# Storing part of one chunk through a second DMA queue, in a fused LoRA linear layer on one core

## The chip, the core and the metric

The kernel runs on one core of one Trainium2 chip. The metric is the device time of one execution in microseconds; the time before is the median of three runs.

## The reference

The inputs are `x` (16 x 2048 x 256, float32), a weight `W` (256 x 256), a low-rank pair `lora_A` (256 x 16) and `lora_B` (16 x 256), a vector `lora_E` of 16 and a scalar `scale`, which is 1.0.

```python
x_flat = x.reshape(-1, in_dim)              # 32768 x 256
y = x_flat @ W
lora_out = x_flat @ lora_A
lora_out = lora_out * lora_E
lora_out = lora_out @ lora_B
y = y + scale * lora_out
return y.reshape(batch, seq_len, out_dim).astype(np.float32)
```

So 33.55 MB are read and 33.55 MB written, and since the low-rank part can be folded into the weight, the rest is one product of a 32768 x 256 matrix with a 256 x 256 matrix.

## The kernel before

The folded weight `weff = W + lora_A (E lora_B) scale` is made once, in bfloat16. The 32768 rows are cut into `N_CHUNKS = 8` chunks of 4 MB. In a chunk each of the 128 SBUF partitions holds `ROWS = 32` rows that follow each other in memory, 1 KB each, so a partition's share of a chunk is one run of 32 KB in DRAM and in SBUF. A chunk lives in one of `N_HOMES = 6` buffers, `home(c)`, into which `x` is loaded and over which `y` is written before it is stored from there. Chunks 6 and 7 take over the buffers of chunks 0 and 1.

Each engine runs its own instruction list, written out by hand with semaphores. A chunk is worked through in 8 groups of 4 rows per partition (`CG = 4`), 64 groups in all:

- SP (SyncE) issues every load and store on one hardware queue, in the order of the list `ORDER`: loads 0 to 5, stores 0 and 1, loads 6 and 7, stores 2 to 7. Load 6 waits until store 0 has landed, load 7 until store 1 has (`stored_of`). A store waits until VectorE has finished its chunk (`s_chunk`). Only the last store, store 7, stands behind the block in which the engines' lists lie (`tc.tile_critical`), and SP reaches it when all engines have come to the end of that block.
- Pool (GpSimd) casts a group from its home into `stage` (bfloat16). Behind its last group it waits for the transposes (`s_turned`), drains, and raises `s_stage` once more.
- TensorE transposes the staged group (`turn`) and multiplies the group before it with `weff` (`multiply`). Since a group is multiplied after the next one has been turned, the last group of a chunk waits for the next chunk's first.
- ScalarE copies the transposed group from PSUM into `xt`, and VectorE copies the product from PSUM over the group in its home.

The lines that the change touches are SP's store branch (L119 to L120) and the end of Pool's list (L143 to L144); the last store is at L229, the exit of the block at L218, and the end of the program at L260.

Of the kernel before, what the change touches and what calls it, by code (L numbers as in the profile page):

```python
# [13 lines left out]
ROWS = 32  # L14
# [5 lines left out]
    "L0", "L1", "L2", "L3", "L4", "L5",  # L20
    "S0", "S1", "L6", "L7", "S2", "S3", "S4", "S5", "S6", "S7",
]

CG = 4
GPC = ROWS // CG
# [8 lines left out]
def kernel(  # L34
# [20 lines left out]
    y_chunks = out_flat.rearrange("(c p b) m -> c p b m", p=P, b=ROWS)  # L55

    sbuf, psum, sem = nc.alloc_sbuf_tensor, nc.alloc_psum_tensor, tc.alloc_semaphore
# [15 lines left out]
    for c in range(N_CHUNKS):  # L73
        s = 0
# [5 lines left out]
    stored_of = {c: sem(f"stored_{c}") for c in range(N_CHUNKS - N_HOMES)}  # L80
    stored_rest = sem("stored_rest")
# [6 lines left out]
    s_y = sem("multiplied")  # L88
    s_free = sem("y_free")
    s_chunk = sem("chunk_done")  # L90

    def home(c):
        return homes[c % N_HOMES]

    sync, gpsimd, scalar, vector, tensor = nc.sync, nc.gpsimd, nc.scalar, nc.vector, nc.tensor

    def sync_program():
        def load(pc):
            c, s, e = pc
            if c >= N_HOMES:  # L100
                sync.wait_ge(stored_of[c - N_HOMES], 16)
            sync.dma_start(out=home(c)[:, s:e, :], in_=x_chunks[c, :, s:e, :]).then_inc(loaded[pc], 16)

        load(pieces[0])
        for name, to, of in (
            ("w", w_sb, W.rearrange("(q t) m -> q t m", t=KT)),
            ("a", a_sb, lora_A.rearrange("(q t) r -> q t r", t=KT)),
            ("e", e_sb, lora_E[:, None]),
            ("b", b_sb, lora_B),
        ):  # L110
            sync.dma_start(out=to[:], in_=of).then_inc(set_up_loaded[name], 16)
        for step in ORDER[:-1]:
            c = int(step[1:])
            if step[0] == "L":
                for pc in pieces:
                    if pc[0] == c and pc != pieces[0]:
                        load(pc)
            else:
                sync.wait_ge(s_chunk, c + 1)  # L119
                sync.dma_start(out=y_chunks[c], in_=home(c)[:]).then_inc(stored_of.get(c, stored_rest), 16)  # L120

    def gpsimd_program():
        gpsimd.memset(ident[:], 0.0).then_inc(s_ident, 1)  # L123
        gpsimd.wait_ge(s_ident, 1)
        gpsimd.affine_select(  # L125
            out=ident[:],
            in_=ident[:],
            compare_op=ALU.not_equal,
            fill=1.0,
            base=0,  # L130
            pattern=[[-1, P]],
            channel_multiplier=1,
        ).then_inc(s_ident, 1)
        for g in range(N_GROUPS):
            c, b = g // GPC, g % GPC * CG
            for pc in pieces:
                if pc[0] == c and pc[1] == b:
                    gpsimd.wait_ge(loaded[pc], 16)
            if g >= NS:
                gpsimd.wait_ge(s_turned, g - NS + 1)  # L140
            gpsimd.tensor_copy(out=stage[g % NS][:], in_=home(c)[:, b:b + CG, :]).then_inc(s_stage, 1)  # L141

        gpsimd.wait_ge(s_turned, N_GROUPS - NS + 1)  # L143
        gpsimd.drain().then_inc(s_stage, 1)  # L144

    def scalar_program():
        for g in range(N_GROUPS):
            scalar.wait_ge(s_turned, g + 1)
            if g >= NX:
                scalar.wait_ge(s_y, g - NX + 1)  # L150
            halves = psum_xt[g % NT][:].bitcast(BF16).rearrange("q b (p t) -> q b t p", t=KT)
            scalar.copy(out=xt[g % NX][:], in_=halves).then_inc(s_xt, 1)  # L152
# [65 lines left out]
    with tc.tile_critical(no_gpsimd_drain=True):  # L218
        sync_program()
        gpsimd_program()  # L220
        scalar_program()
        vector_program()
        tensor_program()
# [41 lines left out]
```

## Time and profile before

| What | Value |
|---|---|
| median of 3 runs | 164.91 us (164.75 to 165.03) |
| profiled execution, own time | 165.03 us |
| its span | 163.24 us |
| DMA queue of SP: packets, MB, share of 16 engines | 2944, 67.41, 96.7% |
| HBM read, written | 33.85 MB, 33.55 MB |
| busy: PE, VectorE, ScalarE, Pool | 60%, 49%, 40%, 41% |
| stores issued by SP at | 29.05, 40.37, 83.55, 84.03, 84.50, 98.25, 110.55, 122.18 us |
| loads 6 and 7 issued at | 73.00, 83.17 us |

The span runs from the first to the last instruction; the execution's own time is 1.79 us longer. The profile lists busy time of each engine, waits with what ended them, DMA queues by packets and bytes, and the share of time in which the core's 16 DMA engines were busy. A DMA is cut into packets; each of the engines it uses works through its own packets one after another and counts up the transfer's semaphore once when it is done, so a transfer over 16 engines leaves 16 landing records in the trace. A packet is shown with its start, its duration and its size, but without the number of its engine.

### The profile page before, as it was taken

The page shows a single profiled execution, that of the slowest core. Times are in us where ns is not written, and L with a number is a line of the kernel's source. Part 1 is how long each engine was busy: PE and PEld are TensorE (multiplying, and loading weights), DVE is VectorE, ACT ScalarE, POOL GpSimd, SP SyncE. Part 2 cuts the span into 40 slices and gives each one's busy share as a digit, 9 for nine tenths or more (in the row PEclk, how much of TensorE's full clock was granted, in tenths as well). Part 3 has the DMA queues.
Part 4 walks back from the last instruction along what each step waited for, and adds up shares of the span by engine and source line. Part 5 has one row for each costly group of instructions (what it writes and reads, how often), then busy time and mean ns, then how long its engine had stood idle before and what let it go on. Part 6 is the DMA issues. An engine that isn't in the chain of part 4 may idle for free. (4 is left out here: it accounts for less than half of the span.)

```text
span 163.2 us, 2145 instructions
## 1 busy us (share of the span) xinstructions
PE 98.3 (60%) x778; PEld 81.7 (50%) x778; DVE 79.5 (49%) x66; ACT 66.1 (40%) x65; POOL 67.1 (41%) x70
## 2 busy tenths in 40 slices
PE   0399938999999999999920099999950000000000
PEld 0268827888888888888810078888840000000000
DVE  0116961888888888888850026888870000000000
ACT  3045723767777676767720026676720000000000
POOL 1445516767777677777400256677400000000000
PEclk9999996999999999999995558999995555555555
DMA  5999998998998999999999999999999999999980
GB/s 163 412 458 454 393 506 385 426 474 385 466 434 385 498 401 387 393 474 420 418 466 393 442 450 393 468 426 418 450 418 426 458 401 458 442 401 466 418 385 16
DMA packets 2948, 67.43 MB, mean 413 GB/s; under 512 B 497, under 2 KB 513, under 8 KB 641
## 3 DMA queue, kind: packets, MB, share of 16 engines
q1 hardware_dynamic: 2944, 67.41, 96.7%
q14 instruction: 4, 0.02, 0.0%
HBM read 33.85 MB, written 33.55 MB: 413 GB/s over the span
## 5 line engine op out<-in xcount | busy, mean ns | idle before, releaser
L171 DVE COPY home<-psum_y 128x1024 f32<-128x1024 f32 x64 | 78.4, 1225 | 32.3 <-PE psum_y L192 29.6
L141 POOL CAST stage<-home 128x1024 bf16<-128x1024 f32 x64 | 66.4, 1041 | 48.3 <-DMA home<-in_x_dram 24.5
L152 ACT COPY xt<-psum_xt 128x1024 bf16<-128x1024 bf16 x64 | 64.8, 1012 | 52.2 <-PE psum_xt L184 52.2
L192 PE MATMUL psum_y<-weff,xt 128*128 128x256 bf16 x512 | 69.8, 281 | 0.9
L192 PEld LDWEIGHTS psum_y<-weff,xt 128*128 128x128 bf16 x512 | 47.9, 101 | 14.6 <-issue 7.1
L184 PE MATMUL psum_xt<-ident,stage 128*128 128x128 f32 x260 | 42.0, 287 | 14.5 <-PEq L177 14.5
L184 PEld LDWEIGHTS psum_xt<-ident,stage 128*128 128x128 f32 x260 | 32.7, 149 | 16.6 <-issue 15.6
L204 PE MATMUL psum_y<-ident,a_sb 128*16 128x128 f32 x2 | 0.6, 394 | 6.8 <-DMA a_sb<-in_lora_A_dram 6.8
L157 DVE TENSOR_SCALAR ate<-psum_y,e_sb 16x256 f32<-16x256 f32 x1 | 0.5, 471 | 7.5 <-PE psum_y L204 7.5
L204 PEld LDWEIGHTS psum_y<-ident,a_sb 128*16 128x16 f32 x2 | 0.1, 90 | 6.8 <-issue 6.8
L210 PE MATMUL psum_y<-b_sb,ate 16*128 16x256 f32 x4 | 2.1, 670 | 0.0
L167 DVE TENSOR_TENSOR weff<-w_sb,psum_y 128x512 bf16<-128x512 f32 x1 | 0.7, 689 | 2.4 <-PE psum_y L210 2.4
L152 ACT ACT_TABLE_LOAD x1 | 1.3, 1283 | 0.9 <-SPq L218 0.9
L210 PEld LDWEIGHTS psum_y<-b_sb,ate 16*128 16x128 f32 x4 | 1.2, 319 | 0.5 <-issue 0.3
L123 POOL MEMSET ident<- 128x128 f32 x1 | 0.2, 205 | 0.5 <-SPq L218 0.5
L125 POOL TENSOR_SCALAR_AFFINE_SELECT ident<-ident 128x128 f32<-128x128 f32 x1 | 0.3, 293 | 0.2 <-POOL ident L123 0.2
L246 POOL MEMSET const-float32-0.0<- 128x1 f32 x1 | 0.1, 98 | 0.2 <-issue 0.2
L246 POOL MEMSET const-bfloat16-1.0<- 128x1 bf16 x1 | 0.1, 101 | 0.0
L246 POOL MEMSET const-uint8-127<- 128x1 uint8 x1 | 0.1, 101 | 0.0
L246 POOL MEMSET const-float32-1.0<- 128x1 f32 x1 | 0.1, 98 | 0.0
## 6 DMA issues: line engine op xcount, KB each, us to landing
out_dram<-home SPq DMA_DIRECT2D x8, 4096.0 KB, 42.4
home<-in_x_dram SPq DMA_DIRECT2D x7, 4096.0 KB, 28.5
home<-in_x_dram SPq DMA_DIRECT2D x2, 1024.0 KB, 5.2
home<-in_x_dram SPq DMA_DIRECT2D x1, 2048.0 KB, 10.0
w_sb<-in_W_dram SPq DMA_DIRECT2D x1, 256.0 KB, 5.1
a_sb<-in_lora_A_dram SPq DMA_DIRECT2D x1, 16.0 KB, 4.8
e_sb<-in_lora_E_dram SPq DMA_DIRECT2D x1, 0.1 KB, 4.5
b_sb<-in_lora_B_dram SPq DMA_DIRECT2D x1, 16.0 KB, 3.9
```

The lines of the kernel that those rows point to most:

```text
L123: gpsimd.memset(ident[:], 0.0).then_inc(s_ident, 1)
L125: gpsimd.affine_select(out=ident[:], in_=ident[:], compare_op=ALU.not_equal, fill=1.0, base=0, pattern=[[-1, P]], channel_multiplier=1,).t ...
L141: gpsimd.tensor_copy(out=stage[g % NS][:], in_=home(c)[:, b:b + CG, :]).then_inc(s_stage, 1)
L152: scalar.copy(out=xt[g % NX][:], in_=halves).then_inc(s_xt, 1)
L157: vector.tensor_scalar(out=ate[:], in0=psum_y[0][:R, :KT, :P], scalar1=e_sb[:], scalar2=float(scale), op0=ALU.mult, op1=ALU.mult,).then_in ...
L167: vector.tensor_add(out=weff[:], in0=w_sb[:], in1=psum_y[1][:, :KT, :]).then_inc(s_free, NY)
L171: vector.tensor_copy(out=home(c)[:, b:b + CG, :], in_=psum_y[g % NY][:]).then_inc(s_free, 1)
L184: ins = tensor.transpose(psum_xt[i % NT][:, b, :], words[:, b, :], ident[:])
L192: ins = tensor.matmul(psum_y[i % NY][:, b, :], xt[i % NX][:, b, t, :], weff[:, t, :], start=(t == 0), stop=(t == KT - 1),)
L204: ins = tensor.transpose(psum_y[0][:R, t, :P], a_sb[:, t, :], ident[:])
L210: ins = tensor.matmul(psum_y[1][:, t, :], ate[:, t, :], b_sb[:], start=True, stop=True)
L246: nc = _bacc.Bacc("TRN2", target_bir_lowering=False, num_devices=1)
```

## The change

Chunk 5's store (the sixth chunk, `SHARED = 5`) is split. The 32 rows of a partition are seen as two halves of 16 (`HALF`); of each half SP's store keeps the first 11 rows (`HEAD`), and the last 5 of each half, 10 rows or 10 KB of a partition, are stored by other transfers:

- partitions 0 to 4 (`BEFORE = 5`) and 5 to 124 (`AROUND = 120`) by two transfers that Pool issues on its own software queue, at the end of its list;
- partitions 125 to 127 by a transfer of SP's, issued ahead of its store of the 22 rows.

Pool then waits until its own two transfers have landed (`s_shared`) and until SP's small one has (`s_rest`), before it leaves the block. The order of SP's other transfers is as before.

```diff
+SHARED = 5
+HALF, HEAD = ROWS // 2, 11
+BEFORE, AROUND = 5, 120
...
+    s_shared = sem("shared_stored")
+    s_rest = sem("rest_stored")
...
                 sync.wait_ge(s_chunk, c + 1)
-                sync.dma_start(out=y_chunks[c], in_=home(c)[:]).then_inc(stored_of.get(c, stored_rest), 16)
+                y_c, home_c = y_chunks[c], home(c)[:]
+                if c == SHARED:
+                    y_c, home_c = (
+                        t.rearrange("p (h b) m -> p h b m", b=HALF) for t in (y_c, home_c)
+                    )
+                    rest = BEFORE + AROUND
+                    sync.dma_start(out=y_c[rest:, :, HEAD:], in_=home_c[rest:, :, HEAD:]).then_inc(s_rest, 16)
+                    y_c, home_c = y_c[:, :, :HEAD], home_c[:, :, :HEAD]
+                sync.dma_start(out=y_c, in_=home_c).then_inc(stored_of.get(c, stored_rest), 16)
...
         gpsimd.drain().then_inc(s_stage, 1)
+        gpsimd.wait_ge(s_chunk, SHARED + 1)
+        y_c, home_c = (
+            t.rearrange("p (h b) m -> p h b m", b=HALF) for t in (y_chunks[SHARED], home(SHARED)[:])
+        )
+        for s, e in ((0, BEFORE), (BEFORE, BEFORE + AROUND)):
+            gpsimd.dma_start(out=y_c[s:e, :, HEAD:], in_=home_c[s:e, :, HEAD:]).then_inc(s_shared, 16)
+        gpsimd.wait_ge(s_shared, 32)
+        gpsimd.wait_ge(s_rest, 16)
```

## The prediction

> **What bounds the kernel now.** I read the page's slices first: the DMA row stands at 8 and 9 tenths from the second slice to the last but one, while every compute engine is idle from about 122 us. The queue rows name the work.
>
> ```profile
> DMA packets 2948, 67.43 MB, mean 413 GB/s; under 512 B 497, under 2 KB 513, under 8 KB 641
> q1 hardware_dynamic: 2944, 67.41, 96.7%
> q14 instruction: 4, 0.02, 0.0%
> ```
>
> One queue, SP's, moves everything. Then the stretches (span, five engines' busy time, clock, DMA share, GB/s), because an average hides how it ends:
>
> ```profile
> core 0: us, PE busy (x) PEld busy (x) DVE busy (x) ACT busy (x) POOL busy (x), PEclk, DMA share, GB/s
> 62.50:82.50 20.00, 19.73 (x172) 16.68 (x170) 17.40 (x15) 14.43 (x15) 13.13 (x13) 1.00 0.99 426
> 105.00:122.00 17.00, 15.41 (x133) 12.81 (x131) 14.70 (x12) 10.19 (x11) 8.45 (x9) 1.00 1.00 432
> 122.00:140.00 18.00, 0.00 (x0) 0.00 (x0) 0.00 (x0) 0.00 (x0) 0.00 (x0) 0.53 1.00 433
> 158.90:160.10 1.20, 0.00 (x0) 0.00 (x0) 0.00 (x0) 0.00 (x0) 0.00 (x0) 0.50 0.07 27
> 160.10:161.80 1.70, 0.00 (x0) 0.00 (x0) 0.00 (x0) 0.00 (x0) 0.00 (x0) 0.50 0.04 19
> ```
>
> Until 158.9 the 16 engines are full; then 27 GB/s is one engine's rate (433 / 16 = 27). The DMA view from 160.1 us to the end confirms that a single engine is left, with one 32 KB packet and its completion write:
>
> ```profile
> DMA packets 2, 0.03 MB, mean 10 GB/s; under 512 B 1, under 2 KB 1, under 8 KB 1
> ```
>
> The trace's landing records give the size: of the last store's 16 completion counts, 15 come between 159.30 and 160.08 us, the last at 162.26. One engine is 2.18 us late, and the program ends 0.98 us after it (163.24).
>
> Where does it fall behind? Packets of one engine follow each other end to start. A 32 KB packet takes 1213 ns, but one engine shows some 14 in a row of about 1286 ns from 64.6 to 82.7 us and 13 more from 105.2 to 121.9: about 27 x 73 ns = 2.0 us. Both stretches have stores in flight and compute running; from 122 us, without compute, its packets are back at 1213. The other fifteen stay at 1213 there. The three runs lie within 0.28 us of each other, so I take the lag to be in each.
>
> Last, the end of Pool's and SP's lists, in the timeline (start, length):
>
> ```profile
> 115.38 1.04 POOL L141 CAST stage<-home 128x1024 bf16<-128x1024 f32 x1 [0.31 <-PE psum_xt L184]
> 98.25 0.33 SPq L120 DMA_DIRECT2D out_dram<-home  x1
> 122.18 0.33 SPq L229 DMA_DIRECT2D out_dram<-home  x1
> ```
>
> and in SP's own waits (total, times, longest):
>
> ```profile
> SPq L218 <- DVEq L218: 10.9, 1, 10.9
> SPq L260 <- DMA out_dram<-home: 39.8, 1, 39.8
> ```
>
> Chunk 5's store is issued at 98.25; the last store at 122.18, after SP has waited at the end of the critical block for every engine. It lands 40.1 us later: it stands that long in the queue. A queue with no idle time ends with its latest engine, so only two things can move the end: how much the late engine carries, and a last store issued so late that the queue runs dry.
>
> **The change part by part.** *Packet sizes.* A 4 MB transfer is 128 packets of 32 KB, 8 per engine, 9.70 us. The trace has 8 KB packets at 309 ns; with 1213 ns for 32 KB that is 37.7 ns per KB plus 8 ns per packet. Chunk 5's rows now lie in two halves: 11 KB runs (422 ns) by SP's store, 5 KB runs (196 ns) in the part cut off. An engine that carries 8 partitions of both has 16 x 422 + 16 x 196 = 9.89 us: +0.19.
>
> *The part cut off* is 10 KB of each partition: 120 partitions go in one Pool transfer, 5 in another, 3 by SP. On 15 engines the 120 make 8 each, as before; the sixteenth has only 16 x 422 = 6.75 us, -2.95. The other 8 partitions cost 2 x 196 = 0.39 us each on whatever engines they land on: I allow none to two per engine, 0 to 0.78.
>
> *If the engine left out is the late one:* it lands at 162.26 - 2.95 = 159.31, with two extras 160.09. The others end at 160.08 + 0.19 = 160.27, with two extras 161.05. They decide, so the gain is 162.26 - 160.27 = 1.99 down to 1.21 us. Eight extras over sixteen engines make one on the latest of them the middle: 160.66, a gain of 1.60.
>
> *Is it that one?* The trace has no Pool transfer and numbers no engine. Each load's landings come in nearly one order, and followed back to 59 us, where it was still undisturbed, the late engine is fourth or fifth of sixteen. If that order is the engines' and the two Pool transfers are dealt out in a ring from the first engine, the 5 take the first five and the 120 all but the fifth. That speaks for it, weakly. [...]
>
> [...]
>
> *New waits.* Pool comes to its first added wait after its drain at 116.86; chunk 5 was done before 98.25, so that one is open. It then issues two transfers (SP's issues take 0.33 to 0.70 us; Pool's are not in the trace: I allow up to 3 us) and waits for its own two and for SP's 3 partitions. Nothing of Pool's own is queued behind that, but SP's wait at the block's end is, and so the last store. What covers it: chunk 6 fills the queue until it lands at 149.6, and from issue to first packet SP's first load took 1.0 us (0.94 to 1.96), so up to 148.6 us the delay costs nothing; beyond that, each us costs one. Pool's transfer shares each engine with a full SP queue. Instruction fetches (q14, 8 KB, at 62.4, 74.3 and 102.1 us) slip in between two 32 KB packets, so I let the queues take turns packet by packet: 16 x (1.213 + 0.196) = 22.5 us from about 120, ending near 143. If a turn takes all 16 pieces it ends near 125. SP's 3 partitions land behind chunk 4, whose store lands by 133.3, plus at most the 3.1 us of Pool's share. All inside 148.6, with some 6 us to spare at the worst of these.
>
> *On SP:* one more issue of some 0.4 us at 98.25, with the queue full: nothing; uncovered it would be 0.4. *The end:* after the last landing the program took 0.98 us; two more semaphores and a used Pool queue may make it 0 to 0.3 more; I take 0.1, since none of it is data.
>
> Sum: the profiled execution's own time is 165.03, of which 163.24 is the span and 1.79 lies around it. 165.03 - 1.60 + 0.10 = 163.5; that execution is 0.12 above the median of the three runs, so against the median 163.4.
>
> **The rivals.** *The engine left out is not the late one.* The late one carries 8 x 10 KB in other packets: +0.19, up to +0.97 with two extras. 165.03 + 0.19 to 0.97 = 165.2 to 166.0, against the median mostly 165.1 to 165.6. For it: nothing in the trace ties the 120 partitions to an engine; were it pure chance it would be 15 in 16. Against it: the place in the landing order, which the 5 partitions' share of the ring would meet.
>
> *Pool's wait holds the last store back (slower).* If a 5 KB run goes out as two pieces and each waits its turn, 32 x (1.213 + 0.102) = 42 us from 120 is 162; the last store is then issued 13 us after the queue has run dry (148.6), and ends at 162 + 1.0 + 9.7 + 0.4 = 173, 11 us late: 176. It decides from a Pool wait ending at 148.6. Against it: SP's pieces show up whole, up to 32 KB, and 10 KB packed in larger turns makes it earlier, not later.
>
> *Late only under compute, and moved.* Another engine could fall behind once Pool's queue works beside SP's between 120 and 143 us; compute ends at 122, so at 73 ns a packet that is two packets, 0.15 us. Inside the range.
>
> **How the numbers follow.** About 0.2% (0.33 us) is what a measurement of this kernel can tell from no change. The late engine left out: 0.66, 162.9 to 163.9, all faster. Another left out: 0.25; about two thirds of it above 165.24, the rest within 0.33 us of the median. Last store late: 0.06, slower. The rest, 0.03, I give to slightly faster or the same. Faster 0.67, same 0.10, slower 0.23. The range for 8 in 10 takes in the first case and most of the second: 162.9 to 165.6; the first case's own is 162.9 to 163.9.
>
> **What would show it.** Right: the last store's 16 landings within about 1.5 us of each other, near 160.7 on the span; a Pool queue of 1.2 MB in the queue rows; fifteen engines with its packets and the engine with the 1286 ns packets without them; Pool's added waits ended, and the last store issued, before 148.6. Wrong: one landing still over 2 us behind, or two engines apart from the rest, one early and one late; a stretch of low DMA share before the last store's packets; or a packet of 5 KB far above 196 ns.

## The result and the profile after

The changed kernel is slower: 166.52 us median of 4 runs (166.28 to 166.77) against 164.84 us for the kernel before (164.75 to 165.03, 4 runs), a ratio of 1.0101 with a 95% interval of 1.0081 to 1.0120. The forecast was 163.4 us in a range of 162.9 to 165.6. The profiled execution took 166.39 us, its span 164.60; as before, 1.79 us lie around the span.

The queue rows of the page show that the change does what it says: 1.28 MB have moved to Pool's queue.

```profile
DMA packets 3404, 67.43 MB, mean 410 GB/s; under 512 B 569, under 2 KB 585, under 8 KB 969
q1 hardware_dynamic: 3081, 66.13, 95.1%
q0 software_dynamic: 320, 1.28, 2.4%
q14 instruction: 3, 0.02, 0.0%
```

The stretches of the changed kernel, in the columns shown in the prediction (the last three are granted clock, DMA share and GB/s):

```profile
105.00:122.00 17.00, 15.81 (x137) 13.18 (x134) 14.77 (x13) 10.59 (x11) 10.27 (x11) 1.00 1.00 432
122.00:131.00 9.00, 0.00 (x0) 0.00 (x0) 0.17 (x1) 0.00 (x0) 0.00 (x0) 0.61 1.00 414
131.00:143.00 12.00, 0.00 (x0) 0.00 (x0) 0.00 (x0) 0.00 (x0) 0.00 (x0) 0.50 1.00 361
143.00:159.00 16.00, 0.00 (x0) 0.00 (x0) 0.00 (x0) 0.00 (x0) 0.00 (x0) 0.50 1.01 436
160.10:161.80 1.70, 0.00 (x0) 0.00 (x0) 0.00 (x0) 0.00 (x0) 0.00 (x0) 0.50 0.63 270
```

The engines are never idle (share 1.00), yet from 131 to 143 us they move 361 GB/s instead of 437: packets take longer. And at 160.1 us, where one engine was left before, most are still at work. The kernel before has in the same stretch:

```profile
131.00:143.00 12.00, 0.00 (x0) 0.00 (x0) 0.00 (x0) 0.00 (x0) 0.00 (x0) 0.50 1.01 437
```

The timeline of the changed kernel has Pool's two transfers and the last store (start, length), and SP's waits name who held the latter back:

```profile
118.06 1.42 POOL L166 DMA_DIRECT2D out_dram<-home  x2 [1.23 <-PE psum_xt L208]
142.44 0.34 SPq L253 DMA_DIRECT2D out_dram<-home  x1
```

```profile
SPq L242 <- POOLq L242: 19.9, 1, 19.9
```

The wait of 19.9 us is real and costs nothing: the last store is issued at 142.44, and the DMA share is 1.01 from 143 to 159 us.

The trace's records of single packets say where it went. From 122 us on, the 5 KB packets take 250 ns in the mean (196 undisturbed), SP's 11 KB packets 488 (422), and some 32 KB packets more than 1213; all together 34.8 us too much, 2.17 us per engine: 13.5 us of it on 5 KB packets and 21.3 on SP's own 11 KB and 32 KB ones. The median packet is undisturbed, at 196 and 422 ns; 53 of Pool's 250 took over 230 ns, up to 826. The last store's 16 landings now lie between 161.40 and 163.62 us: no engine is 2 us behind all others any more, but the first fifteen have moved from a mean of 159.66 to 162.25.

### The profile page after: what moved, and what is told of

Read it like the earlier page. It is cut to its first block, busy times and chain, and to the rows that moved or that the text cites. A ratio compares the mean times of both kernels' runs of the same rounds, so it can differ in the third digit from the quotient of the medians.

```text
span 164.6 us, 2150 instructions
## 1 busy us (share of the span) xinstructions
PE 99.2 (60%) x778; PEld 82.5 (50%) x778; DVE 79.5 (48%) x66; ACT 66.1 (40%) x65; POOL 68.5 (42%) x72
## 3 DMA queue, kind: packets, MB, share of 16 engines
q0 software_dynamic: 320, 1.28, 2.4%
## 5 line engine op out<-in xcount | busy, mean ns | idle before, releaser
L208 PE MATMUL psum_xt<-ident,stage 128*128 128x128 f32 x260 | 42.7, 291 | 13.8 <-PEq L201 13.8
L166 POOL DMA_DIRECT2D out_dram<-home x2 | 1.4, 712 | 1.2 <-PE psum_xt L208 1.2
```

The lines of the kernel that those rows point to most:

```text
L166: gpsimd.dma_start(out=y_c[s:e, :, HEAD:], in_=home_c[s:e, :, HEAD:]).then_inc(s_shared, 16)
L208: ins = tensor.transpose(psum_xt[i % NT][:, b, :], words[:, b, :], ident[:])
```

## The experiments

Each edit is against the changed kernel; `POOL_PARTS` and `SP_PARTS` list the partitions whose cut-off rows are stored by Pool and by SP ahead of its 22-row store, one transfer each, in place of (0, 5), (5, 125) and (125, 128). The counts that Pool waits for at its end follow the number of transfers; these lines are left out below. The kernel before was timed beside them; ratios are to it.

**Small runs, second queue, or the deal over 15 engines?** Three kernels cut the same rows into the same runs and change only who stores them.

```diff
 # e1
+POOL_PARTS, SP_PARTS = (), ((0, 128),)
 # e2
+POOL_PARTS, SP_PARTS = ((0, 128),), ()
 # e3
+POOL_PARTS, SP_PARTS = (), ((0, 120), (120, 128))
```

All by SP over 128 partitions (e1):

> Chunk 5's rows are cut into the same 11 KB and 5 KB runs, but SP stores both parts, each over all 128 partitions; Pool issues nothing. Theory PORTS (Pool's transfer reads a partition through another DMA engine than SP's stores do, so two engines meet on one partition's way out): no stretched packets, every engine +0.19 us, the late engine still 2 us behind, 164.9 to 165.2 us. Theory TURNS (two queues alternating on one engine cost time): the same, 164.9 to 165.2. Theory SMALL (runs of 5 and 11 KB are slow to write into HBM): packets stretched as in the changed kernel (5 KB mean 250 ns, 11 KB mean 488 ns), 166.5 to 167.5.

Measured 164.82 us, ratio 0.9998 (0.9987 to 1.0010). Every 5 KB packet took 196 ns and every 11 KB packet 422. SMALL falls.

All by Pool over 128 partitions (e2):

> Pool stores the 10 rows of all 128 partitions in one transfer, 8 partitions on each of 16 engines; SP's small transfer is gone. The two queues still meet on every engine. PORTS: if a 128-partition Pool transfer is dealt to the engines as SP's is, no engine meets another's partitions; 5 KB packets near 196 ns, 11 KB near 422, the late engine not relieved: 164.9 to 165.3 us. TURNS: stretched as in the changed kernel, all engines +2 us, the late one too: 166.5 to 167.5. SMALL: the same as TURNS, 166.5 to 167.5.

Measured 164.94 us, ratio 0.9997 (0.9982 to 1.0013); again 196 and 422 ns without exception, though each engine alternates between the queues. TURNS falls. Its stretch, beside the 361 GB/s above:

```profile
131.00:143.00 12.00, 0.00 (x0) 0.00 (x0) 0.00 (x0) 0.00 (x0) 0.00 (x0) 0.50 1.03 438
```

The late engine stays late here (160.42 for the fifteenth landing, 162.24 for the last), and the time with it.

By SP, 120 partitions and 8 (e3):

> The 10 rows go by SP's queue, 120 partitions in one transfer over 15 engines and the last 8 in another; Pool issues nothing. One queue, but the 120 partitions are dealt out over 15 engines, otherwise than the other stores. PORTS: stretched packets while the 120-partition transfer runs, mean of the 5 KB packets above 230 ns, 0.5 to 3 us lost, 165.5 to 168. TURNS: no stretching, +0.2 to +0.6 for the extra partitions, 165.0 to 165.6. SMALL: 166.5 to 167.5.

Measured 169.24 us median; the four runs spread from 166.09 to 169.50, which I can't explain. The trace is of an execution of 169.31, so it is a hint and no more: 5 KB packets 276 ns in the mean, 11 KB 442, 1.74 us per engine too much, without Pool. The first 49 packets of 5 KB all took 196 ns, stretched ones come from 131.07 us on. So a second queue costs nothing by itself (e2), and e3 suggests that the deal of the 120 partitions does; that it costs on either queue is not shown.

**Is it the late engine that is left out?**

```diff
-BEFORE, AROUND = 5, 120
+POOL_PARTS, SP_PARTS = ((0, 4), (4, 124)), ((124, 128),)
```

> As the changed kernel, but the two Pool transfers take 4 and 120 partitions and SP's small one 4. If Pool's transfers are dealt round a ring of 16 from the first engine, the fourth engine is now left out instead of the fifth, and the late engine carries its full share again: one landing of the last store 1.5 to 3 us behind the rest, 167.3 to 168.7 us. If the place of the left-out engine does not depend on the 5, the time stays at the changed kernel's 166.5 within 0.3. PORTS, TURNS and SMALL do not differ here.

Measured 166.96 us, ratio 1.0110 (1.0084 to 1.0136); 2.51 us per engine too much, the last landings at 164.06 and 164.57. That lies between the two expected times, and not apart from the changed kernel's. The packets are clear, though: the engine with the run of some 1286 ns packets before 122 us carries two 5 KB packets in the changed kernel, one partition of the transfer of 5, and 16 here. The 5 does decide who is left out, and it picks the late engine.

**DRAM or SBUF?** Two kernels send the rows of chunk 5 to other places in DRAM, one with each deal: first the 22-row parts of all partitions one behind the other (`flat[:cut]`), then the 10-row parts.

```diff
+        flat = y_c.rearrange("p b m -> (p b) m")
+        cut = P * 2 * HEAD
...
+            flat[:cut].rearrange("(p h b) m -> p h b m", p=P, h=2),
+            flat[cut:].rearrange("(p h b) m -> p h b m", p=P, h=2),
...
 # e5
+POOL_PARTS, SP_PARTS = ((0, 128),), ()
 # e6
+POOL_PARTS, SP_PARTS = ((0, 5), (5, 125)), ((125, 128),)
```

> As the kernel in which Pool stores the 10 rows of all 128 partitions, but the rows go to another place in DRAM: SP's 22-row parts of chunk 5 one behind the other, then Pool's 10-row parts (the rows of chunk 5 come out in another order). SBUF side as there, DRAM side shifted against the engines. PORTS on the SBUF side: still no stretched packets (5 KB 196 ns, 11 KB 422), 164.7 to 165.2 us. PORTS on the DRAM side: now stretched, 5 KB mean above 220 ns, 166 to 168.

> The changed kernel's 5, 120 and 3 partitions with the same moved place in DRAM. PORTS on the SBUF side: stretched as in the changed kernel (5 KB mean 240 to 260 ns, 11 KB 460 to 500), 166.2 to 167.2 us. PORTS on the DRAM side: the stretching differs clearly from the changed kernel's, in either direction, since every place in DRAM is another.

e5: 165.14 us, ratio 1.0011 (0.9993 to 1.0030), no packet stretched. e6: 166.85 us, ratio 1.0107 (1.0074 to 1.0140), 5 KB 246 ns, 11 KB 491, 2.44 us per engine. With either deal the packets are as they were with the old places, so the place in DRAM is not the cause. What is left to try is where in SBUF the fifteen engines read. The stretch of e6:

```profile
131.00:143.00 12.00, 0.00 (x0) 0.00 (x0) 0.00 (x0) 0.00 (x0) 0.00 (x0) 0.50 0.99 351
```

**Half the rows.**

```diff
-HALF, HEAD = ROWS // 2, 11
+HALF, HEAD = 32, 27
```

> The changed kernel with half the rows cut off: the last 5 of the 32 in one run of 5 KB, SP's part one run of 27 KB. PORTS: half as much meets, so half of the changed kernel's loss on the other engines (some 1.0 to 1.8 us instead of 2.1 to 3.5) and half of the late engine's relief; they would end together near 161.8, 164.0 to 164.9 us. If the loss does not go with the amount (a fixed cost of starting Pool's queue): 166 to 166.7.

Measured 165.12 us, ratio 1.0012 (0.9996 to 1.0027). The loss fell to 0.58 us per engine, a quarter where half was expected, and the last landing is at 162.89, 1.4 us behind the fifteenth. The trace shows why: the late engine carries nine of Pool's packets, one of the transfer of 5 and eight of the 120. With one run per partition in place of two, another engine was left out, so this run says nothing on the relief, and its time lies in neither of the expected ranges.

**Who meets whom?**

```diff
 # e8
+POOL_PARTS, SP_PARTS = ((0, 32),), ()
 # e9
+HALF, HEAD = 8, 3
+POOL_PARTS, SP_PARTS = ((0, 16),), ()
```

> Pool stores the 10 rows of partitions 0 to 31 alone, 2 partitions on each of 16 engines; those of partitions 32 to 127 are not stored, so 0.98 MB less is written. PORTS: 16 engines meet on a quarter of the partitions, so the 5 KB packets are stretched more than in the changed kernel, mean above 300 ns; without stretching the late engine would land at 160.1 and the execution take 162.9 us. If only the number of small packets counts, 64 of them instead of 256 are stretched less, mean at most 250 ns.

> Pool stores 20 rows (four runs of 5 KB) of partitions 0 to 15 alone, one partition on each of 16 engines: 64 packets of 5 KB, as many as with 32 partitions. SP's store of chunk 5 keeps 12 rows in 3 KB runs; the other 20 rows of partitions 16 to 127 are not stored, 2.3 MB less. GROUP (several engines share the way out of a small group of neighbouring partitions): 16 engines crowd on a few groups, most of the 64 packets stretched, mean above 400 ns. PARTITION (only two engines on the very same partition hinder each other): each engine meets at most one other, for about an eighth of the time, at most a quarter of the packets stretched, mean below 260 ns.

e8: 162.87 us, 7 of the 64 packets stretched, mean 214 ns: my 300 was wrong. e9: 159.89 us, 17 of 64, mean 263, at PARTITION's end of the scale but between the two. Neither settles it: in the changed kernel before 131 us a 32 KB packet of 1213 ns lies between two of an engine's Pool packets of 196, and if that is so here too, few of them are under way at once (an estimate).

So e10 takes the stores away from beside the transfer:

```diff
                 if c == SHARED:
+                    sync.wait_ge(s_shared, 32)
...
         gpsimd.wait_ge(s_chunk, SHARED + 1)
+        gpsimd.wait_ge(stored_rest, 48)
```

> The changed kernel, but Pool's two transfers start only when the stores of chunks 2 to 4 have landed, and SP issues nothing more until they have landed: Pool's 120 partitions run with nothing beside them. MEETING (a packet is stretched when Pool's engine and the engine that carries the same partition for SP are there at once): no stretched 5 KB packet, mean below 205 ns. DEAL (the deal over 15 engines is slow in itself, its own engines hinder each other): still stretched, mean above 230 ns. The time is longer in both, by the waits, 168 to 176 us.

173.95 us, and 291 ns in the mean with nothing beside it. MEETING falls as the whole cause: Pool's engines hinder each other. What slowed SP's packets in the changed kernel, with 21.3 of its 34.8 us, this run can't say. Of the 250 packets 117 took 194 to 205 ns and 53 took 365 to 390, about twice the time; the others lie between and above, up to 778. The stretch, with the engines busy and the rate low:

```profile
135.60:139.60 4.00, 0.00 (x0) 0.00 (x0) 0.00 (x0) 0.00 (x0) 0.00 (x0) 0.50 0.89 252
```

The transfer of 5, which ran ahead of the 120, shows that neighbours hinder each other too: of its five engines, which read partitions 0 to 4, one had both its packets at about 200 ns (202 and 196), and the other four took 264 to 778 ns; 4 x 196 is 784. So four of the five, on partitions that are neighbours, at the worst took as long as four packets in turn. Which partition the undisturbed one read the trace does not show.

Two kernels put chunk 2 in place of chunk 5, on MEETING's account:

```diff
-SHARED = 5
+SHARED = 2
 # e12 also
+HALF, HEAD = 32, 27
```

> The changed kernel with chunk 2 in place of chunk 5: SP's 22-row store of chunk 2 is long done when Pool sends the 10 rows, beside SP's full 32 KB packets of later chunks. MEETING: two engines now walk the partitions out of step, so they meet by chance only, as in the changed kernel before 131 us: some 85 ns per Pool packet in place of 139, 1.3 us lost per engine in place of 2.2; 164.6 to 165.8 us. If what matters is only that 250 packets go by the wrong engines: 166.2 to 166.8 as in the changed kernel.

> Chunk 2 and half the rows, 5 in one run: half of 1.3 us lost, half of the relief kept. MEETING: others land near 161.1, the late engine between 160.9 and 161.9, 163.9 to 164.8 us, a little faster than before. Otherwise as with chunk 5 and five rows, 165.0 to 165.3.

e11: 166.91 us, ratio 1.0127 (1.0101 to 1.0153), 5 KB packets 252 ns, 2.33 us per engine too much: no less than the changed kernel, so walking in or out of step with SP's store of the same rows makes no difference. The loss on SP's side, 23.1 us in all, here lies on its 32 KB packets. e12: 164.94 us, ratio 1.0009 (0.9994 to 1.0023); it has one run per partition, as e7, and the late engine carries Pool's packets here too. Its trace shows one engine with none of them, five with nine and ten with eight.

**Which partitions meet?** Alone again, as e10, with 60 partitions, 4 to each of 15 engines, in two places: if any deal over 15 engines is slow, both are; if it matters which partitions are read, they can differ.

```diff
 # e13
+POOL_PARTS, SP_PARTS = ((32, 92),), ()
 # e14
+POOL_PARTS, SP_PARTS = ((0, 60),), ()
```

> Pool stores the 10 rows of partitions 32 to 91 alone, 60 partitions, 4 on each of 15 engines, with nothing beside it; the other partitions' 10 rows are not stored. [...] DEAL (any deal over 15 engines is slow): mean above 250 ns as with 120 partitions. The time is no test.

> The same with partitions 0 to 59. [...] DEAL: mean above 250 ns, as with partitions 32 to 91.

e13: 120 packets, mean 200 ns, none over 211: DEAL falls. e14: mean 331, 86 of 120 between 360 and 380 ns, and one engine whose eight packets all took 196. The trace does not number it. If the shares are fours in order and hinder each other at one fixed distance, an estimate from that one engine gives the distance: at 32 partitions just one of the fifteen shares, 28 to 31, has no other that far away, and at no other multiple of four is it just one. The same bytes over as many engines, in the two stretches in which the transfers ran:

```profile
135.40:137.20 1.80, 0.00 (x0) 0.00 (x0) 0.00 (x0) 0.00 (x0) 0.00 (x0) 0.50 0.84 341
```

```profile
135.40:138.70 3.30, 0.00 (x0) 0.00 (x0) 0.00 (x0) 0.00 (x0) 0.00 (x0) 0.50 0.76 186
```

Partitions 32 to 91 (first) leave in 1.8 us, 0 to 59 in 3.3. Two engines with a 5 KB packet each in some 370 ns move 27.7 GB/s together, where one with a packet in 196 ns moves 26.1; so, if they meet in pairs, a pair got little more than one engine's rate. The distance of 32 is not enough for that: e13's shares in 32 to 59 also have others 32 partitions away, in 64 to 91, and ran clean. So, as far as the estimate of the distance holds, partitions 32 apart hinder each other within 0 to 59 (e14, 331 ns in the mean), and not from 32 to 59 to 64 to 91 (e13, 200 ns); of 64 to 127 alone there is no run, and why it is so no run shows. The changed kernel's 120 partitions, in shares of eight in order, have such pairs: 5 to 12 with 37 to 44, for example. How 128 partitions are dealt, so that e1, e2 and e5 had no stretched 5 KB or 11 KB packet, no run here shows.

**Does the late engine end by what it carries?** First with four partitions alone, by the ring on other engines than the late one, in two places:

```diff
 # e15
+POOL_PARTS, SP_PARTS = ((16, 20),), ()
 # e16
+POOL_PARTS, SP_PARTS = ((20, 24),), ()
```

> SP stores 22 rows of chunk 5 for all partitions; the other 10 rows are stored by Pool for partitions 16 to 19 alone, in one transfer of 4 partitions on 4 other engines than the late one, 40 KB; for all other partitions they are not stored. [...] ENGINE-BOUND: the late engine carries none of it; the same time as with partitions 20 to 23, within 0.3 us.

> The same with partitions 20 to 23. [...]

e15: 161.74 us, ratio 0.9808 (0.9778 to 0.9837); e16: 162.19, ratio 0.9833 (0.9804 to 0.9863). Without any of the cut-off rows the late engine should land at 162.26 - 9.70 + 6.75 = 159.3 us, 162.1 in all with the 0.98 and 1.79 us behind it and around the span: e16's last landing is at 159.34, and neither run is later than that sum by more than 0.1 us. So the 40 KB on other engines did not hold the late one up, as ENGINE-BOUND has it. e16's 0.45 us more than e15, over the 0.3 that ENGINE-BOUND allowed, is not explained (it has one 32 KB packet of 1705 ns).

Then directly, with e13's clean shares beside SP's stores:

```diff
 # e17
+POOL_PARTS, SP_PARTS = ((0, 5), (32, 92)), ()
 # e18
+POOL_PARTS, SP_PARTS = ((0, 4), (32, 92)), ()
```

> SP stores 22 rows of chunk 5; of the other 10 rows Pool stores those of partitions 0 to 4 (a transfer of 5) and of 32 to 91 (60 over 15 engines, the late one left out), beside SP's stores; the rest of them is not stored. RELIEF (an engine ends by what it carries): the late engine has 22 rows and one partition of Pool's, lands at 162.26 - 2.95 + 0.39 = 159.7 us, the others at most at 160.08 - 2.95 + 1.57 + 0.39 = 159.1 plus stretching; 162.3 to 162.7 us in all, and 0.9 to 1.4 us less than with the fourth engine left out. NO RELIEF: the same time as that one within 0.3 us. If Pool's shares meet SP's engines, 5 KB packets are stretched here although they do not meet each other, mean above 215 ns; if only Pool's own meet, below 205.

> The same with a first transfer of 4 partitions (0 to 3), so that the late engine carries its share of the 60: four partitions, 1.57 us. RELIEF: it lands at 162.26 - 2.95 + 1.57 = 160.9 us, 163.5 to 163.9 us in all. NO RELIEF: as with the late engine left out, within 0.3 us.

e17: 162.27 us (162.21 to 162.32), ratio 0.9859 (0.9843 to 0.9875); e18: 163.37 (163.23 to 164.00), ratio 0.9935 (0.9910 to 0.9959). RELIEF holds: 1.10 us between them, expected 0.9 to 1.4. The late engine carries two 5 KB packets in e17 and eight in e18; six packets of 196 ns are 1.18 us, and the last landings lie 1.13 us apart. The DMA view of the two from 158.6 us to the end, e17 first, shows the last 32 KB packet of a single engine in e18 alone:

```profile
DMA packets 3, 0.00 MB, mean 0 GB/s; under 512 B 3, under 2 KB 3, under 8 KB 3
```

```profile
DMA packets 4, 0.03 MB, mean 6 GB/s; under 512 B 3, under 2 KB 3, under 8 KB 3
```

And hardly anything is stretched: 5 KB packets 196.7 and 196.4 ns in the mean, 0.03 us per engine too much, beside SP's stores. The stretch of e17, where the changed kernel had 361 GB/s:

```profile
131.00:143.00 12.00, 0.00 (x0) 0.00 (x0) 0.00 (x0) 0.00 (x0) 0.00 (x0) 0.50 1.03 438
```

Both kernels leave out rows, so their times compare with each other only.

| Kernel | Pool's partitions | 5 KB packets, mean ns | too much, us per engine | 15th and last landing, us | ratio |
|---|---|---|---|---|---|
| before | none | none | 0 | 160.08, 162.26 | 1 |
| changed | 0-4, 5-124 | 250 | 2.17 | 163.53, 163.62 | 1.0101 |
| e2 | 0-127 | 196 | 0 | 160.42, 162.24 | 0.9997 |
| e4 | 0-3, 4-123 | 247 | 2.51 | 164.06, 164.57 | 1.0110 |
| e17 | 0-4, 32-91 | 197 | 0.03 | 159.27, 159.44 | 0.9859, rows left out |
| e18 | 0-3, 32-91 | 196 | 0.03 | 158.99, 160.57 | 0.9935, rows left out |

## Why the prediction was wrong

*The term that failed* is the price of the part cut off. It took 196 ns for a 5 KB packet and 422 for an 11 KB packet as given, from an undisturbed 8 KB and 32 KB packet, and bounded only how many single partitions each engine gets. It never asked whether fifteen engines with other shares than SP's can all read at full rate. They can't: alone on the queues, fifteen shares in 0 to 59 took 331 ns a packet in the mean (e14) where those in 32 to 91 took 200 (e13), and by the estimate from e14 the changed kernel's 120 partitions have pairs like those of e14. In the changed kernel a 5 KB packet of Pool's took 250 ns in the mean and an 11 KB packet of SP's 488. The term's size: 0.19 us on every engine for the cut itself, some 0.2 for the single partitions (eight of 0.39 over 15 engines), and 2.17 for the stretching: 159.66 + 0.19 + 0.2 + 2.17 = 162.2, where the fifteen landed at 162.25. With this term the mean comes out. The last but one landed later still, at 163.53 in place of 160.27 to 161.05, since the stretching is uneven over the engines.

*The bound was too narrow for an operation that the trace did not show.* The range for the 120 partitions took only counts from 0 to 0.97 us, with no end for a slower packet, and no rival had it, although a 5 KB packet far above 196 ns stands among the signs of being wrong. Two engines at half rate would have been a natural far end: 16 x 196 ns once more, 3.1 us.

*What held:* the engine left out is the late one (two Pool packets on it in the changed kernel, 16 in e4), although the evidence for it was weak, its place in the landing order, and was called so. The ring assumed there fits this, but not the packets of e7 and e12 (nine on the late engine in e7; in e12 one engine with none, five with nine): with one run per partition the same 5 and 120 left out another engine. Its relief is real: 1.10 us between e17 and e18. The landing 2 us behind is gone. In the changed kernel, however, the others' loss of 2.6 us is more than the 2.18 that there was to gain.

*Pool's wait* cost nothing, as reckoned: the queues took turns packet by packet (1213, 196, 1213 and 196 ns follow each other on one engine from 127.02 us), the last store was issued at 142.44, before 148.6, and the queue never ran dry. That the landing at 142.14 is so near the reckoned 143 is luck. The sum had a 32 KB packet in each of SP's turns, but from about 131 us on SP's turns are mostly 11 KB packets; in e2, with as many clean 5 KB packets on each engine, Pool's transfer landed by 138.29. The stretching made up the rest. *The end* took 0.98 us after the last landing, as before; the 0.1 us added there was not needed.

*The rivals.* "The engine left out is not the late one" gave a time nearer to the result, but for a reason that did not occur; the last store was not late; and of the third, another engine that falls behind while compute runs, the changed kernel's trace shows nothing: the run of some 1286 ns packets is on one engine again.

*Left open.* Pool's shares beside SP's stores were hardly stretched in e17 (196.7 ns in the mean), and yet 21.3 of the changed kernel's 34.8 us fell on SP's packets. Even the late engine, with two of Pool's packets, landed at 161.40 or later there, where the prediction had 159.31 to 160.09. So Pool's shares are shown to slow each other (e14, 331 ns in place of 196), but how they slow SP's packets beside them is not shown, and the picture does not price every meeting; e3, whose first 49 packets were clean, is not explained by it either. Why one engine's store packets take 1286 ns while compute runs was not tried. Nor was a complete kernel whose fifteen shares keep clear of each other: e17 does so only by leaving rows out, and no full version measured here beats the kernel before.

## What to carry to other kernels

When a transfer is dealt to the engines otherwise than its neighbours, look at which partitions the engines read at the same time before pricing its packets: here 60 partitions over 15 engines took 331 ns per 5 KB packet in 0 to 59 and 200 ns in 32 to 91 (e14, e13). In a profile whose DMA share is 1.00 throughout, compare GB/s stretch by stretch and the mean duration of each packet size: at a share of 1.00 these engines moved 361 GB/s where they had moved 437. Ending all engines together, here worth 1.10 us between e17 and e18 and 2.18 at the most, pays only if the rearrangement costs the others less than that; here it cost them 2.6.

## What the runs showed of the hardware

- A Pool store of partitions 0 to 59 over 15 engines, alone on the queues, took 331 ns per 5 KB packet in the mean, 86 of 120 between 360 and 380, with one engine at 196 throughout (e14); one of partitions 32 to 91 took 200 in the mean and at most 211 (e13). Of five engines on partitions 0 to 4, four took 264 to 778, and one 202 and 196 (e10).
- With Pool's 5 KB and SP's 11 KB packets on the same engines, all took 196 and 422 ns in e2 and e5: the second queue cost nothing there.
- Which engine a 120-partition Pool transfer leaves out depends on what went before it (with 5 partitions the late engine carried two 5 KB packets, with 4 it carried 16), and changed when each partition's part was one run instead of two (nine packets of a run each on the late engine, e7).
